# Two-layer decoder trunk: the last part of each feed-forward way down by eight products, chunk by chunk

## The chip, the cores and the metric

One core of one Trainium2 chip runs the whole program as a single launch. The metric is device microseconds of that core. The time before is the median of 3 runs; the profile is of one more execution.

## The reference, cut to what matters

The program computes two layers of a decoder trunk over 512 positions of width 1024, all in float32. Each layer adds to the residual x a mixer (layer 0: sliding-window and stick-breaking attention; layer 1: HGRN2, a gated linear recurrence), then a cross-attention to 256 memory rows, and then a feed-forward net. The change is in the last of these:

```python
def conv_ffn(h, w_up, conv_w, conv_b, w_down):
    S = h.shape[1]
    u = h @ w_up                                   # 1024 -> 2 * 2816
    shift = lambda t, n: jnp.pad(t, ((0, 0), (n, 0), (0, 0)))[:, :S]
    u = sum(conv_w[CONV_WIDTH - 1 - n] * shift(u, n) for n in range(CONV_WIDTH)) + conv_b
    gate, up = jnp.split(u, 2, axis=-1)
    return (jax.nn.silu(gate) * up) @ w_down       # 2816 -> 1024

for l in range(2):
    ...
    x = x + conv_ffn(rms_norm(x, norm_ffn[l]), ffn_w_up[l], ffn_conv_w[l], ffn_conv_b[l], ffn_w_down[l])
```

`h @ w_up` is the way up, `@ w_down` the way down. The inner width 2816 is 22 chunks of 128.

## The kernel before, in words

**Layout.** The residual lives transposed: `xT[c]` holds channels 128c to 128c+127 on the partitions and the 512 positions along the row (8 chunks; `xT2` joins two chunks in one tile). Every float32 operand of a product is split in two parts: `hi` (a cast to fp32r on ScalarE, `A.copy`) and `lo = x - hi` (on VectorE); see `split`. A product is then three matmuls: hi·hi, hi·lo and lo·hi (`mm3`, L183 to L185; in `seven_part` all three stand in L349).

**Weights.** `wload` loads a tile of 256 columns by DMA from SyncE's queue into `wraw` (two buffers), and splits it into `whi` and `wlo` (two buffers each) at L171 and L172. The buffers of one tile come free when the last matmul that reads them is done.

**Way up.** `ffn` walks over m = 0 to 10, two inner chunks at a time: `gate_half(m)` and `value_half(m)` each multiply the normed input with one weight tile (`proj_fm`: two outputs j = 0, 1 of 128x512 in the PSUM tile `ps_pj`, three buffers, 24 matmuls each, k in order). The evacuation of one output is `half`: times the row norm into `fu` (VectorE, L613), first tap and bias into `fa` (ScalarE, L615), two more taps (VectorE, L616 and L618); then the gate's Silu, or for the value the product with the gate (VectorE, L638).

**Way down.** The 22 inner chunks are cut into three parts, `parts = [(0, 8), (8, 16), (16, 22)]`, and after each part its share of the way down is added to the residual. It is done with seven block products in place of eight: the pair of chunks of one m and the two halves of 256 positions make a 2x2 block, `seven` builds the seven right operands of it (`s7h` and `s7l`, with sums in `s7t`; L318 to L321, and splits in L213 and L214), and `seven_part` builds the seven left operands from the weights (`wr`, `wraw`, sums in `wsum`, L353, splits L213 and L214), multiplies (L349: 128x128 by 128x256) into the PSUM tiles `ps_at`, `ps_ov` and `ps_pj`, and adds the results into `xT2` (`into`, L366). It does so in two units of four output chunks. For the last part (`fill` is false, since no gate half follows) the first unit takes another order of the seven products, with the last k held back.

**After the way down.** In layer 0 the next mixer follows. Its `norm` takes the chunks of xT one by one: scale and split into `xh` and `xl` (L235, L236, two instructions each, since this norm is folded), squares (ScalarE), their sum `nacc` (GpSimd, L246, the last one on VectorE); `Norm.finish` makes of the sum the factor of each position and spreads it by a matmul (L256, L266). The projections of the mixer read xh and xl chunk by chunk. At the same time GpSimd builds seven masks (L1075 to L1081). In layer 1 the way down is the end of the program: `store(sp, c)` transposes chunk c (TensorE, L436), copies it to `ot` (two buffers; ScalarE for even c, VectorE for odd, L441 and L439) and writes it out by DMA (L442).

**Order.** The framework orders each engine's instructions ahead of time with a planner of its own (`schedule_with_timeline_sim=True`): among the instructions that its reckoned times show as ready, it takes the earliest in the program. On the chip each engine then keeps that order.

`proj_resid`, which the attention's and the HGRN2's output projections use, is the plain way: for each of four weight tiles of 256 columns two outputs of 128x512, each the sum over all k, added to one chunk of xT (L297), and then, where given, a function `after(c)`.

Of the kernel before, what the change touches and what calls it, by code (L numbers as in the profile page):

```python
# [11 lines left out]
FP32R = mybir.dt.float32r  # L12
I32 = mybir.dt.int32
AF = mybir.ActivationFunctionType
ALU = mybir.AluOpType
# [3 lines left out]
P = 128  # L19
# [7 lines left out]
FC = DFF // P  # L27
# [6 lines left out]
def trunk(ctx, tc, x, mem, positions, norm_mix, norm_cross, norm_mem, norm_ffn,  # L34
# [13 lines left out]
    def tl(pool, shape, tag, bufs=1, dt=FP32):  # L48
        return pool.tile(shape, dt, name=tag, tag=tag, bufs=bufs)
# [22 lines left out]
    def f32(ap):  # L72
        return ap.bitcast(FP32)
# [138 lines left out]
    def split(src, hi, lo, eng=None):  # L212
        A.copy(out=hi, in_=src)  # L213
        V.tensor_tensor(out=lo, in0=src, in1=f32(hi), op=ALU.subtract)  # L214
# [109 lines left out]
        split(t, hi[:, 3:7], lo[:, 3:7])  # L324
        return hi, lo

    def seven_part(w, r0, xs, sp, sums, fill, after=None):


        n = len(xs)  # L330
        nk = 2 * n
        side = [None, 0]

        def weights(src):
            if side[1] == 0:
                side[0] = tl(wp, [P, KC, WCOL], "whi", 2, FP32R), tl(wp, [P, KC, WCOL], "wlo", 2, FP32R)
            h, lo = (t[:, side[1] * n:(side[1] + 1) * n] for t in side[0])
            side[1] = 1 - side[1]
            split(src, h, lo)
            return h, lo  # L340

        def product(o, wt, slot, first, ks=None):
            wh, wl = wt
            for k in range(n) if ks is None else ks:
                xh, xl = xs[k][0][:, slot], xs[k][1][:, slot]
                for j in range(2):
                    c = slice(j * P, (j + 1) * P)
                    for i, (p, q) in enumerate(((wh, xh), (wh, xl), (wl, xh))):
                        T.matmul(o[:, j], lhsT=p[:, k, c], rhs=q, start=first and k == 0 and j == 0 and i == 0,  # L349
                                 stop=k == n - 1 and j == 1 and i == 2, skip_group_check=True)  # L350

        def add(out, p, q):
            V.tensor_tensor(out=out, in0=p, in1=q, op=ALU.add)  # L353

        def unit(u, fill):
            raws = []
            for i in range(2):
                raw = tl(sp if i == 0 else wp, [P, KC, WCOL], "wr" if i == 0 else "wraw", 1 + i)
                SY.dma_start(out=raw[:, :nk], in_=wcols(w, r0, nk * P, (4 * u + 2 * i) * P))
                raws.append(raw)  # L360
            a11, a12 = (raws[0][:, i:nk:2] for i in range(2))
            a21, a22 = (raws[1][:, i:nk:2] for i in range(2))

            def into(i, th, o, op):
                x = xT2[2 * u + i][:, :, 256 * th:256 * th + 256]
                V.tensor_tensor(out=x, in0=x, in1=o, op=op)  # L366

            ws = tl(sp, [P, KC // 2, WCOL], "wsum", sums)[:, :n]
            al, be, de = ps("at", 2, WCOL), ps("ov", 2, WCOL), ps("pj", 2, WCOL)
            w11 = weights(a11)  # L370
            if not fill:
                w12 = weights(a12)
                product(al, w11, 0, True, range(n - 1))
                product(be, w12, 1, True, range(n - 1))
                product(al, w11, 0, True, range(n - 1, n))
                product(be, w12, 1, True, range(n - 1, n))
                add(ws, a21, a22)
                into(0, 0, al, ALU.add)
                into(0, 0, be, ALU.add)
                w1 = weights(ws)  # L380
                add(ws, ws, a11)
                w2 = weights(ws)
                product(al, w2, 4, False)
                product(de, w1, 3, True)
                add(ws, ws, a12)
                into(0, 1, al, ALU.add)
                into(1, 1, de, ALU.subtract)
                add(a21, a11, a21)
                w3 = weights(a21)
                w4 = weights(ws)  # L390
                product(al, w3, 5, False)
                product(de, w4, 2, False)
                w22 = weights(a22)
                into(1, 1, al, ALU.subtract)
                into(0, 1, de, ALU.add)
            else:
                add(ws, a21, a22)
                w1 = weights(ws)
                product(al, w11, 0, True)
                product(de, w1, 3, True)  # L400
                add(ws, ws, a11)
                w2 = weights(ws)
                into(0, 0, al, ALU.add)
                product(al, w2, 4, False)
                add(ws, ws, a12)
                w4 = weights(ws)
                into(1, 1, de, ALU.subtract)
                product(de, w4, 2, False)
                add(a21, a11, a21)
                w3 = weights(a21)  # L410
                into(0, 1, al, ALU.add)
                product(al, w3, 5, False)
                w12 = weights(a12)
                into(0, 1, de, ALU.add)
                product(be, w12, 1, True)
                w22 = weights(a22)
                into(1, 1, al, ALU.subtract)
                into(0, 0, be, ALU.add)
            product(al, w22, 6, False)
            if after is not None:  # L420
                for c in (4 * u, 4 * u + 1):
                    after(c)
            into(1, 0, al, ALU.subtract)
            if after is not None:
                for c in (4 * u + 2, 4 * u + 3):
                    after(c)

        unit(0, fill)
        unit(1, True)

    ov = out[0].rearrange("(t p) d -> p t d", p=P)

    def store(sp, c):
        pt = ps("at" if c % 2 else "tr", NT, P)
        for t in range(NT):
            T.transpose(out=pt[:, t], in_=xT[c][:, t * P:(t + 1) * P], identity=ident)  # L436
        ot = tl(sp, [P, NT, P], "ot", 2)
        if c % 2:
            V.tensor_copy(out=ot, in_=pt)  # L439
        else:  # L440
            A.copy(out=ot, in_=pt)  # L441
        SY.dma_start(out=ov[:, :, c * P:(c + 1) * P], in_=ot)  # L442
# [163 lines left out]
    def ffn(l, xp, sp):  # L606
        n = norm(gains("ffn", l), xtiles(xp))
        xh, xl, rb = n.xh, n.xl, n.rb
        parts = [(0, 8), (8, 16), (16, 22)]

        def half(o, ch):
            u = tl(sp, [P, S], "fu", 2)
            V.tensor_tensor(out=u, in0=o, in1=rb, op=ALU.mult)  # L613
            a = tl(sp, [P, S], "fa", 6)
            A.activation(out=a, in_=u, func=AF.Identity, scale=conv_col(l, 2, ch), bias=bias_col(l, ch))  # L615
            V.scalar_tensor_tensor(out=a[:, 1:], in0=u[:, :S - 1], scalar=conv_col(l, 1, ch), in1=a[:, 1:],  # L616
                                   op0=ALU.mult, op1=ALU.add)
            V.scalar_tensor_tensor(out=a[:, 2:], in0=u[:, :S - 2], scalar=conv_col(l, 0, ch), in1=a[:, 2:],  # L618
                                   op0=ALU.mult, op1=ALU.add)
            return a  # L620

        hs = {}

        def gate_half(m):
            gt = [None, None]

            def evg(j, o):
                a = half(o, 2 * m + j)
                A.activation(out=a, in_=a, func=AF.Silu)
                gt[j] = a  # L630
            wg = wload(wcols(ffn_w_up[l], 0, D, m * WCOL))
            proj_fm(wg, xh, xl, evg, n.finish if m == 0 else None, after_rows(n) if m == 0 else None)
            return gt

        def value_half(m, gt):
            def evu(j, o):
                a = half(o, FC + 2 * m + j)
                V.tensor_tensor(out=a, in0=gt[j], in1=a, op=ALU.mult)  # L638
                gt[j] = a
                if j:  # L640
                    hs[m] = seven(sp, sp, gt[0], gt[1], 4)
            wu = wload(wcols(ffn_w_up[l], 0, D, DFF + m * WCOL))
            proj_fm(wu, xh, xl, evu)


        gt = gate_half(0)
        for a, b in parts:
            for m in range(a // 2, b // 2):
                value_half(m, gt)
                gt = gate_half(m + 1) if 2 * m + 2 < FC else None  # L650
            seven_part(ffn_w_down[l], a * P, [hs[m] for m in range(a // 2, b // 2)], sp, 2 - l, gt is not None,
                       (lambda c: store(sp, c)) if l == 1 and b == FC else None)

    first_norm = []

# [601 lines left out]
    for l in range(2):  # L1257
# [3 lines left out]
        sp, sp_close = pool(f"xa{l}", "left")  # L1261
# [9 lines left out]
        sp, sp_close = pool(f"ffn{l}", "right")  # L1271
# [29 lines left out]
```

## Time and profile before

| what | value |
|---|---|
| runs | 1616.61, 1621.70, 1620.54 us; median 1620.54 |
| the profiled execution | 1618.11 us, its span 1616.3 us |
| TensorE clock granted, mean | 0.992 |
| TensorE (PE) busy | 1576.8 us, 98% |
| VectorE (DVE) busy | 1164.2 us, 72% |
| ScalarE (ACT) busy | 761.1 us, 47% |
| GpSimd (POOL) busy | 196.2 us, 12% |

All times inside the profile count from the start of the span. Busy TensorE time is the union of modelled matmul durations that overlap one another: matmuls start closer together than they last, so costs below are taken from the distance of their starts. "Granted clock" is the share of its full clock that TensorE was given in a stretch.

### The profile page before, as it was taken

How to read it: one execution, taken by the hardware profiler on the slowest of the kernel's cores; microseconds unless marked ns; L12 is line 12 of the kernel's file. 1: busy time of each engine (PE TensorE's matmuls, PEld its weight loads, DVE VectorE, ACT ScalarE, POOL GpSimd, SP SyncE). 2: the span in 40 equal slices, each digit the busy share in tenths (PEclk: the TensorE clock that was granted, in tenths of full speed). 3: DMA queues.
4: the chain of work that ended last, by engine and by line, in shares of the span. 5: the costliest groups of instructions: out<-in, count | busy, mean ns of one | idle time of the engine just before them, and what ended most of it. 6: DMA issues, size and time to landing. Idle time of an engine off the chain costs nothing.

```text
span 1616.3 us, 23124 instructions
## 1 busy us (share of the span) xinstructions
PE 1576.8 (98%) x9182; PEld 1363.9 (84%) x9182; DVE 1164.2 (72%) x1888; ACT 761.1 (47%) x1312; POOL 196.2 (12%) x307
## 2 busy tenths in 40 slices
PE   8999999999999999997999999999999999999997
PEld 7977898887888888987889888988888889889887
DVE  6766976566688779688776677645555988788786
ACT  6576874454443344344433344544543544444332
POOL 3302422002000000001322223101002000000000
PEclk9999999999999999998999999999999999999998
DMA  6211434213322421421322212342204322422312
GB/s 192 79 54 31 129 107 132 79 53 105 104 79 74 135 86 60 136 65 46 105 79 79 78 53 91 119 157 79 78 27 130 105 78 65 145 91 66 124 40 73
DMA packets 144489, 145.71 MB, mean 90 GB/s; under 512 B 2844, under 2 KB 143837, under 8 KB 144381
## 3 DMA queue, kind: packets, MB, share of 16 engines
q1 hardware_dynamic: 143882, 143.98, 27.9%
q8 instruction: 73, 1.20, 0.3%
q0 software_dynamic: 96, 0.07, 0.1%
q14 instruction: 35, 0.29, 0.1%
q10 hardware_dynamic: 403, 0.18, 0.0%
HBM read 142.12 MB, written 2.10 MB: 89 GB/s over the span
## 4 chain that ended last, share of the span: by engine, by line
PE 90%; DVE 4%; ACT 3%; DMA 1%; POOL 1%; issue 0%; SPq 0%; DVEq 0%; ACTq 0%
PE ps_pj L185 23%; PE ps_pj L184 23%; PE ps_pj L183 23%; PE ps_at L349 7%; PE ps_pj L349 3%; PE ps_ov L349 2%; PE ps_at L1123 1%; DVE wlo L214 1%; PE ps_ov L994 1%; ACT whi L213 1%; DVE xl L236 1%; DMA wraw<-in_ab_w_in_dram 1%; PE ps_tr L983 1%; PE ps_at L183 1%; PE ps_at L185 1%; DVE wlo L172 1%
## 5 line engine op out<-in xcount | busy, mean ns | idle before, releaser
L184 PE MATMUL ps_pj<-xl,whi 128*128 128x512 f32 x1088 | 430.5, 396 | 0.0
L185 PE MATMUL ps_pj<-xh,wlo 128*128 128x512 f32 x1024 | 408.5, 399 | 0.0
L183 PE MATMUL ps_pj<-xh,whi 128*128 128x512 f32 x1024 | 406.7, 398 | 0.0
L172 DVE TENSOR_TENSOR wlo<-wraw,whi 128x1024 fp32r<-128x1024 f32 (+1 forms) x228 | 264.2, 1191 | 45.8 <-ACT whi L171 45.2
L171 ACT CAST whi<-wraw 128x1024 fp32r<-128x1024 f32 (+1 forms) x228 | 219.5, 1012 | 161.1 <-PE ps_pj L184 107.9
L184 PEld LDWEIGHTS ps_pj<-xl,whi 128*128 128x128 f32 x1088 | 204.8, 188 | 49.6 <-issue 1.2
L183 PEld LDWEIGHTS ps_pj<-xh,whi 128*128 128x128 f32 x1024 | 192.7, 188 | 44.6 <-issue 1.2
L185 PEld LDWEIGHTS ps_pj<-xh,wlo 128*128 128x128 f32 x1024 | 192.6, 188 | 43.7
L615 ACT ACTIVATE fa<-fu,ccol 128x512 f32<-128x512 f32 x88 | 71.6, 814 | 100.7 <-DVE fu L613 100.5
L185 PE MATMUL ps_pj<-whi,xl 128*128 128x256 f32 x416 | 118.4, 287 | 0.1
L246 POOL TENSOR_TENSOR nacc<-nacc,nsq 128x512 f32<-128x512 f32 x36 | 50.6, 1406 | 540.9 <-ACT nsq L245 540.5
L349 PE MATMUL ps_at<-s7h,whi 128*128 128x256 f32 x352 | 102.7, 292 | 5.8 <-ACT s7h L213 3.4
L349 PE MATMUL ps_at<-s7l,whi 128*128 128x256 f32 x352 | 102.0, 290 | 1.5 <-DVE s7l L214 1.5
L349 PE MATMUL ps_at<-s7h,wlo 128*128 128x256 f32 x352 | 101.8, 290 | 1.3 <-DVE wlo L214 1.3
L184 PE MATMUL ps_pj<-ol,whi 128*128 128x512 f32 x256 | 101.7, 397 | 0.0
L183 PE MATMUL ps_pj<-oh,whi 128*128 128x512 f32 x256 | 99.9, 401 | 1.4 <-DVE xl L478 0.9
L185 PE MATMUL ps_pj<-oh,wlo 128*128 128x512 f32 x256 | 101.2, 397 | 0.0
L613 DVE TENSOR_TENSOR fu<-ps_pj,rb 128x512 f32<-128x512 f32 x88 | 60.7, 689 | 45.7 <-PE ps_pj L185 45.4
L183 PE MATMUL ps_pj<-whi,xh 128*128 128x256 f32 x288 | 82.8, 290 | 0.7 <-ACT xh L235 0.7
L184 PE MATMUL ps_pj<-wlo,xh 128*128 128x256 f32 x288 | 81.9, 286 | 0.0
L185 PEld LDWEIGHTS ps_pj<-whi,xl 128*128 128x128 f32 x416 | 78.5, 190 | 0.6 <-DVE xl L236 0.3
L349 PEld LDWEIGHTS ps_at<-s7h,whi 128*128 128x128 f32 x352 | 69.3, 197 | 7.8 <-ACT s7h L213 3.8
(382 smaller groups left out, 3279.8 us busy)
## 6 DMA issues: line engine op xcount, KB each, us to landing
wraw<-in_ffn_w_up_dram SPq DMA_DIRECT2D x44, 1024.0 KB, 5.1
wraw<-in_xa_w_kv_dram SPq DMA_DIRECT2D x16, 1024.0 KB, 6.0
wraw<-in_hgrn_w_in_dram SPq DMA_DIRECT2D x16, 1024.0 KB, 5.4
wraw<-in_ab_w_in_dram SPq DMA_DIRECT2D x8, 1024.0 KB, 5.4
wraw<-in_xa_w_q_dram SPq DMA_DIRECT2D x8, 1024.0 KB, 5.1
wraw<-in_xa_w_o_dram SPq DMA_DIRECT2D x8, 1024.0 KB, 5.0
wr<-in_ffn_w_down_dram SPq DMA_DIRECT2D x8, 1024.0 KB, 5.2
wraw<-in_ffn_w_down_dram SPq DMA_DIRECT2D x8, 1024.0 KB, 5.0
```

The lines of the kernel that those rows point to most:

```text
L171: A.copy(out=hi[:, k, c], in_=raw[:, k, c])
L172: V.tensor_tensor(out=lo[:, k, c], in0=raw[:, k, c], in1=f32(hi[:, k, c]), op=ALU.subtract)
L183: mm = T.matmul(o, lhsT=lh, rhs=rh, start=first, stop=False)
L184: T.matmul(o, lhsT=lh, rhs=rl, start=False, stop=False)
L185: T.matmul(o, lhsT=ll, rhs=rh, start=False, stop=last)
L213: A.copy(out=hi, in_=src)
L214: V.tensor_tensor(out=lo, in0=src, in1=f32(hi), op=ALU.subtract)
L236: self.last = V.scalar_tensor_tensor(out=b, in0=v, scalar=g, in1=f32(a), op0=ALU.mult, op1=ALU.subtract)
L246: (V if c == KC - 1 else G).tensor_tensor(out=self.acc, in0=self.acc, in1=sq, op=ALU.add)
L349: T.matmul(o[:, j], lhsT=p[:, k, c], rhs=q, start=first and k == 0 and j == 0 and i == 0, stop=k == n - 1 and j == 1 and i == 2, skip_grou ...
L613: V.tensor_tensor(out=u, in0=o, in1=rb, op=ALU.mult)
L615: A.activation(out=a, in_=u, func=AF.Identity, scale=conv_col(l, 2, ch), bias=bias_col(l, ch))
```

## The change

For the last part of each layer (inner chunks 16 to 21, m = 8, 9, 10) `value_half` no longer builds the seven operands; it splits each chunk as it comes into a tile of two chunks, and the way down of that part goes through `proj_resid` with those six chunks. In layer 1 `store` is called for each output chunk after its addition. Parts one and two keep the seven products, in the order that they had. The branch of `seven_part` for a last part, and its `after`, are gone.

```diff
-    def seven_part(w, r0, xs, sp, sums, fill, after=None):
+    def seven_part(w, r0, xs, sp, sums):
...
-            if not fill:
-                w12 = weights(a12)
-                product(al, w11, 0, True, range(n - 1))
-                product(be, w12, 1, True, range(n - 1))
-                product(al, w11, 0, True, range(n - 1, n))
-                product(be, w12, 1, True, range(n - 1, n))
...
-            else:
-                add(ws, a21, a22)
...
+            add(ws, a21, a22)
...
             product(al, w22, 6, False)
-            if after is not None:
-                for c in (4 * u, 4 * u + 1):
-                    after(c)
             into(1, 0, al, ALU.subtract)
-            if after is not None:
-                for c in (4 * u + 2, 4 * u + 3):
-                    after(c)
-
-        unit(0, fill)
-        unit(1, True)
+
+        unit(0)
+        unit(1)
...
                 a = half(o, FC + 2 * m + j)
                 V.tensor_tensor(out=a, in0=gt[j], in1=a, op=ALU.mult)
                 gt[j] = a
-                if j:
+                if m >= last:
+                    if j == 0:
+                        hs[m] = [tl(sp, [P, 7, 256], "s7" + c, 4, FP32R)[:, :4].rearrange("p (a b) c -> p a (b c)", a=2)
+                                 for c in "hl"]
+                    split(a, hs[m][0][:, j], hs[m][1][:, j])
+                elif j:
                     hs[m] = seven(sp, sp, gt[0], gt[1], 4)
...
+        last = parts[-1][0] // 2
         gt = gate_half(0)
         for a, b in parts:
             for m in range(a // 2, b // 2):
                 value_half(m, gt)
                 gt = gate_half(m + 1) if 2 * m + 2 < FC else None
-            seven_part(ffn_w_down[l], a * P, [hs[m] for m in range(a // 2, b // 2)], sp, 2 - l, gt is not None,
-                       (lambda c: store(sp, c)) if l == 1 and b == FC else None)
+            if b < FC:
+                seven_part(ffn_w_down[l], a * P, [hs[m] for m in range(a // 2, b // 2)], sp, 2 - l)
+            else:
+                hh, hl = ([hs[i // 2][q][:, i % 2] for i in range(a, b)] for q in range(2))
+                proj_resid(ffn_w_down[l], a * P, hh, hl, (lambda c: store(sp, c)) if l == 1 else None)
```

More of the change, by code (lines that the diff above doesn't have):

```diff
@@ L340, in weights, with product @@
             return h, lo
-        def product(o, wt, slot, first, ks=None):
+        def product(o, wt, slot, first):
             wh, wl = wt
-            for k in range(n) if ks is None else ks:
+            for k in range(n):
                 xh, xl = xs[k][0][:, slot], xs[k][1][:, slot]
@@ L353, in add, with unit @@
             V.tensor_tensor(out=out, in0=p, in1=q, op=ALU.add)
-        def unit(u, fill):
+        def unit(u):
             raws = []
@@ L370, in unit @@
             w11 = weights(a11)
-            if not fill:
-                w12 = weights(a12)
-                product(al, w11, 0, True, range(n - 1))
-                product(be, w12, 1, True, range(n - 1))
-                product(al, w11, 0, True, range(n - 1, n))
-                product(be, w12, 1, True, range(n - 1, n))
-                add(ws, a21, a22)
[L378 to L395, printed above, removed]
-            else:
[L397 to L418, printed above, removed]
@@ new lines, in unit @@
+            add(ws, a21, a22)
+            w1 = weights(ws)
+            product(al, w11, 0, True)
+            product(de, w1, 3, True)
+            add(ws, ws, a11)
+            w2 = weights(ws)
+            into(0, 0, al, ALU.add)
+            product(al, w2, 4, False)
+            add(ws, ws, a12)
+            w4 = weights(ws)
+            into(1, 1, de, ALU.subtract)
+            product(de, w4, 2, False)
+            add(a21, a11, a21)
+            w3 = weights(a21)
+            into(0, 1, al, ALU.add)
@@ L419, in unit @@
+            product(al, w3, 5, False)
+            w12 = weights(a12)
+            into(0, 1, de, ALU.add)
+            product(be, w12, 1, True)
+            w22 = weights(a22)
+            into(1, 1, al, ALU.subtract)
+            into(0, 0, be, ALU.add)
             product(al, w22, 6, False)
-            if after is not None:
-                for c in (4 * u, 4 * u + 1):
-                    after(c)
             into(1, 0, al, ALU.subtract)
-            if after is not None:
-                for c in (4 * u + 2, 4 * u + 3):
-                    after(c)
```

## The prediction

> **What bounds the kernel now.** I read the page first: the busy times (in the table above) and the chain that ended last.
>
> ```profile
> PE 90%; DVE 4%; ACT 3%; DMA 1%; POOL 1%; issue 0%; SPq 0%; DVEq 0%; ACTq 0%
> ```
>
> TensorE carries 90% of the chain, so a change pays by giving it less to do or fewer waits. Busy time can't say which, since matmuls overlap in it. So next the matmuls of L349 alone, over the two stretches in which the last part goes down (columns: stretch, length, PE busy and count, PEld, granted clock, DMA share, GB/s):
>
> ```profile
> 731.70:776.00 44.30, 36.02 (x252) 34.73 (x251) 0.85 0.21 66
> 1567.40:1607.60 40.20, 34.64 (x252) 32.97 (x251) 0.92 0.16 47
> ```
>
> Both hold the 252 matmuls of seven products (2 units x 7 x 3 pairs x 2 x 3), and neither had the full clock. What one costs when nothing waits is read from starts: in the timeline, the 97 starts of 128x512 matmuls from the first row below to the second; in the chain, a run of 18 of 128x256, then transposes and the end of the program.
>
> ```profile
> 1544.79 0.40 PE L185 MATMUL ps_pj<-xh,wlo 128*128 128x512 f32 x1
> ...
> 1567.19 0.40 PE L185 MATMUL ps_pj<-xh,wlo 128*128 128x512 f32 x1
> ```
>
> ```profile
> 1605.49 2.12 PE ps_at L349 x18
> 1607.61 0.44 PE ps_tr L436 x4
> ...
> 1609.24 2.72 DMA out_dram<-ot
> ...
> 1612.08 0.69 DVE ot L439
> ```
>
> A 512-wide matmul takes (1567.19 - 1544.79) / 96 = 0.2333 us, a 256-wide one 2.12 / 18 = 0.118, a transpose 0.11. The 252 should take 29.7 us. They take 44.3 in layer 0 and 40.2 in layer 1. The waits of TensorE (layer 0 with the start of the next mixer; layer 1; the start of an attention output projection) and the busy times by stage (PE, PEld, DVE, ACT, POOL, then the clock) show the rest:
>
> ```profile
> PE ps_pj L349 <- ACT whi L213: 4.3, 1, 4.3
> PE ps_at L349 <- ACT s7h L213: 2.5, 1, 2.5
> PE ps_tr L266 <- DVE nsq L263: 2.1, 1, 2.1
> ...
> PE ps_at L349 <- DVE wlo L214: 0.2, 1, 0.2
> ```
>
> ```profile
> PE ps_tr L436 <- DVE xT L366: 0.9, 1, 0.9
> ...
> PE ps_ov L349 <- ACT s7h L213: 0.5, 1, 0.5
> ```
>
> ```profile
> PE ps_pj L183 <- ACT oh L213: 0.2, 1, 0.2
> ```
>
> ```profile
> 415.00:427.00 12.00, 12.00 (x52) 9.33 (x51) 8.92 (x12) 7.77 (x9) 0.00 (x0) 1.00 0.19 60
> 676.00:731.70 55.70, 55.70 (x241) 44.79 (x239) 44.34 (x62) 23.16 (x31) 0.00 (x0) 1.00 0.24 80
> 743.00:757.00 14.00, 13.32 (x91) 13.17 (x91) 10.35 (x15) 6.56 (x11) 1.32 (x1) 0.77 0.30 98
> 757.00:770.00 13.00, 8.52 (x53) 8.11 (x52) 11.01 (x15) 5.17 (x10) 2.81 (x3) 0.74 0.06 13
> 792.00:804.00 12.00, 10.32 (x36) 7.60 (x37) 9.21 (x20) 5.13 (x9) 2.24 (x6) 0.86 0.02 5
> 1567.40:1579.50 12.10, 8.97 (x67) 8.03 (x65) 11.87 (x18) 5.61 (x7) 0.00 (x0) 0.98 0.20 65
> 1579.50:1590.40 10.90, 10.85 (x66) 10.60 (x67) 7.63 (x10) 2.40 (x3) 0.00 (x0) 0.71 0.01 2
> 1607.60:1616.30 8.70, 1.89 (x17) 1.50 (x14) 2.07 (x3) 1.17 (x2) 0.00 (x0) 0.82 0.44 121
> ```
>
> The first fence has six rows with 10.4 us, of which 8.3 lie in the way down (2.1 is the next norm's); the second five rows with 4.0. After each series of waits the clock falls: 0.77 of 14 us and 0.74 of 13 us lose 3.2 + 3.4 us, 0.86 of 12 us loses 1.7, 0.71 of 10.9 us loses 3.2. Layer 0 adds up: 29.7 + 8.3 + 6.6 = 44.6. Layer 1: 29.7 + 16 transposes 1.8 + 4.0 + 3.2 = 38.7 of 40.2; 1.5 are in gaps too short to be listed. While TensorE waits, DVE is full: 11.87 of 12.1 us.
>
> **Why it waits there.** Rows of VectorE and ScalarE around the last value chunk:
>
> ```profile
> 1562.03 0.69 DVE L613 TENSOR_TENSOR fu<-ps_pj,rb 128x512 f32<-128x512 f32 x1 [0.88 <-PE ps_pj L185]
> ...
> 1565.17 0.69 DVE L638 TENSOR_TENSOR fa<-fa 128x512 f32<-128x512 f32 x1
> ...
> 1572.60 0.95 DVE L214 TENSOR_TENSOR wlo<-wsum,whi 128x768 fp32r<-128x768 f32 x1
> ...
> 1578.28 1.22 DVE L214 TENSOR_TENSOR s7l<-s7t,s7h 128x1024 fp32r<-128x1024 f32 x1
> ```
>
> ```profile
> 1570.86 0.83 ACT L213 CAST whi<-wsum 128x768 fp32r<-128x768 f32 x1 [1.69 <-DVE wsum L353]
> 1572.72 0.62 ACT L213 CAST s7h<-fa 128x512 fp32r<-128x512 f32 x1 [1.03 <-DVE fa L638]
> ```
>
> An undisturbed evacuation takes 3.8 us from fu to the end of the product with the gate. The last chunk's starts at 1567.6, but its last operand is done at 1579.5: sums and weight splits of 0.95 us stand between. That is what the products wait for.
>
> **The change part by part.**
>
> *Matmuls, both layers.* Out: 252 of 256 wide. In: 8 outputs x 6 k x 3 = 144 of 512 wide, 144 x 0.2333 = 33.6 us. Against 29.7 that is 3.9 us more work in each layer. It stands only against the 44.3 and 40.2 that the seven products really take.
>
> *Vector work, both layers.* Out: 8 sums and 14 splits of weights at 0.95 and 14 additions at 0.69, 30.6 us of DVE, and the operands of three m; in: 8 splits at 0.95 and 8 additions at 0.69, 13.1 us. It costs nothing as long as it lies beside matmuls. Each weight tile feeds 36 matmuls, 8.4 us, in which the next one's two splits (1.9 us DVE, 1.7 ACT) and two additions (1.4) fit. If that cover went, one tile would cost TensorE up to 3.6 us. In the way up before it, TensorE is full (55.70 of 55.70), so fewer operands to build there bring nothing.
>
> *Start of the way down, the term without a row.* The sum over k ends with the last chunk, and that comes 3.8 + 0.2 for the semaphores + 0.62 = 4.6 us after the last value matmul, 5.3 with its lo. Cover: 15 matmuls of the first output (k = 0 to 4) are 3.5 us, 15 of the second 3.5 more, 7.0 in all, and a third PSUM buffer holds the next tile's. The nearest row is the attention output projection, which also waits for its last k: 0.2 us. Bounds: 0, and 4.6 - 3.5 = 1.1 with a slow clock behind (up to 3.2), 4.3. I take 0.4 a layer, nearest to that row. Below nothing is excluded: this wait can't be less than none.
>
> *Layer 0, the next norm.* Chunks 0 to 6 are now finished 4.2 us apart, not four at a time, so their scaling, squares and sums on GpSimd lie beside matmuls. The wait of 2.1 us and the slow clock behind it, 1.7, should go. GpSimd still builds masks there, which can delay the row factors. The nearest row is the feed-forward norm behind an output projection in eight products: 415 to 427 is full at clock 1.00 (that norm isn't folded: half as many scalings). Bounds: gain 3.8, gain 0. I take 3.4, near that row.
>
> *Layer 1, the stores.* Seven chunks' transposes are in the stream: 7 x 0.44 = 3.1 us (four before). Each needs its addition first; the row of before shows one such wait of 0.9. Bounds 0 to 7 x 0.9 = 6.3; I take 0.15 each, 1.0, since DVE is now idle half of the time and matmuls of the next chunk can go ahead. The tail: now 8.7 us, because four chunks' copies queue for two `ot` buffers, and the last copy waits for a DMA of 2.72. Then, chunk 6 is stored 4.2 us ahead, and after the last matmul come: addition 0.1 + 0.69, transposes 0.6, copy 0.69, DMA 2.7, and 0.8 from there to the end of the span (1616.3 - 1612.77 - 2.7), 5.6.
>
> *Queues.* SyncE issues four 768 KB loads as before, now all into `wraw`. The third tile's can go once the first has been split, 8.4 us and more before its use, against this landing time:
>
> ```profile
> wraw<-in_ffn_w_down_dram SPq DMA_DIRECT2D x4, 768.0 KB, 4.4
> ```
>
> So they are hidden; a load queued behind a store of `ot` could be late by that store's wait, but the last load is due before the first store. GpSimd gets the same sums, earlier. `ps_at`, which the stores use, is no longer shared with products.
>
> *The sum.* Layer 0: -44.3 + 33.6 + 0.4 = -10.3, norm -3.4. Layer 1: -40.2 + 33.6 + 3.1 + 0.4 + 1.0 = -2.1, tail 5.6 - 8.7 = -3.1. In all -18.9. From the profiled execution's 1618.1 us that is 1599.2; it was 2.4 below the median of 1620.5, and from there it is 1601.6. I take 1600.
>
> **The rivals.**
>
> *A, the sum above.* 1600, with its own range of 1595 to 1605.
>
> *B, the last chunk's wait stays.* If TensorE's order keeps output after output, each layer waits 1.1 us and pays the slow clock, 4.3 in place of 0.4: +7.8, 1608. For it: the clock fell to 0.71 in layer 1 behind waits of at most 0.9. Against: the row of 0.2 in the same situation. The Trainium skill ("TensorE: Matmul & The Clock Gate", the table of what matters for kernels) says that only idle gaps over about 3 us bring the half clock back; by that rule B would cost 0.7 a layer more than A, 1601, inside A's range. This trace disagrees: 0.71 stands behind waits of 0.9 us, and the measurement decides.
>
> *C, the ends gain nothing.* The norm still waits (+3.4), and each store's transposes wait 0.9 (+5.3): 1609. For it: masks on GpSimd, the row of 0.9. Against: DVE is no longer full.
>
> *D, slower: the weights become the bound.* Each of the 8 weight tiles must be split within 8.4 us behind norm and store work on ScalarE and VectorE. If the planner puts the splits last, a tile is late by its two splits, 3.6 us, and its matmuls run at 0.74 clock behind (8.4 / 0.74 - 8.4 = 3.0): 8 x 6.6 = 53 us, 1652. It decides at 18.9 / 8 = 2.4 us per tile. Against: splits and additions are 3.3 us of 8.4 on VectorE, before two chunks' norm or stores; and 415 to 427, which ends an output projection of the same shape with larger tiles and runs into the next weights, is full.
>
> *E, no change.* The stalls come back in the order of the next mixer, whose instructions are all planned anew: all of 18.9 would have to return. Nothing in the rows speaks for it.
>
> **How the numbers follow.** A 0.74, B 0.10, C 0.08, D 0.04, E 0.04. The runs shown spread over 0.3% (1616.6 to 1621.7), about what can be told from no change; faster by more means under 1615.7. A, B and C are faster: 0.92; E 0.04; D 0.04. The range reaches from A's low end, less 2 us for waits that I don't list, to C: 1593 to 1609, which leaves out D, E and the tails.
>
> **What would show it.** In the changed profile: 288 matmuls of 512 in place of 504 of 256; the last part of layer 0 takes about 34 us at clock 1.00, with a first wait of under 1 us; no wait of L266 for nsq; TensorE's last matmul to the end of the span 5.6 us. I am wrong if TensorE waits several us for the last chunk or for `wlo`, if a slow clock shows in these stretches, or if the mixer of layer 1 takes longer than now.

## The result, and the profile after

| | before | after |
|---|---|---|
| median | 1620.39 us (4 runs, 1616.61 to 1621.70) | 1600.52 us (4 runs, 1599.90 to 1604.62) |
| ratio | | 0.9887, 95% interval 0.9863 to 0.9910 |
| profiled execution, span | 1618.11, 1616.3 us | 1600.87, 1599.2 us |
| mean granted clock | 0.992 | 0.998 |

The change makes the kernel 20 us faster. First the page of the changed kernel, TensorE's busy time and the chain that ended last:

```profile
PE 1575.4 (99%) x8966; PEld 1352.3 (85%) x8966; DVE 1121.5 (70%) x1818; ACT 745.1 (47%) x1294; POOL 199.3 (12%) x307
...
PE 94%; ACT 2%; DVE 1%; DMA 1%; issue 0%; POOL 0%; SPq 0%
```

TensorE's busy time is almost the same (1576.8 before); what went are 4 points of the chain's share on VectorE and ScalarE, and the slow clock of these stages. The stages (length, busy time of PE, PEld, DVE, ACT, POOL, then clock, DMA share and GB/s): way down of layer 0, the start of the next norm, on to the first score matmul, way down of layer 1, tail.

```profile
733.10:767.00 33.90, 33.90 (x146) 27.06 (x146) 25.53 (x35) 17.40 (x31) 7.71 (x5) 1.00 0.35 108
767.00:776.00 9.00, 9.00 (x40) 7.26 (x39) 6.17 (x12) 4.76 (x7) 7.57 (x16) 1.00 0.47 150
776.00:791.40 15.40, 15.40 (x71) 12.22 (x70) 9.25 (x18) 4.89 (x9) 4.47 (x17) 1.00 0.05 9
1556.60:1593.50 36.90, 36.90 (x172) 29.79 (x171) 15.44 (x23) 7.61 (x11) 0.00 (x0) 1.00 0.22 64
1593.50:1599.20 5.70, 1.05 (x8) 0.57 (x6) 1.38 (x2) 0.59 (x1) 0.00 (x0) 0.83 0.32 92
```

TensorE is full in the first four and has its full clock. Where the last part's 0.85 and 0.92 stood there is 1.00. The chain shows how the last chunk's lateness was covered; three first terms of a product in a row, in layer 0 and in layer 1:

```profile
744.09 0.70 PE ps_pj L183 x3
...
1567.58 0.70 PE ps_pj L183 x3
```

These are the sixth k of three outputs at once. They stand 10.7 us after the first matmul of the way down (733.38 and 1556.87), and 45 matmuls of 0.2333 us are 10.5: TensorE had done five of six k for three outputs, one for each PSUM buffer. That is the order that the planner chose, and more cover than was needed: in layer 1 the last chunk's split ends at 1563.09, 6.2 us after the first matmul of the way down and 4 us before its turn (the same 6.2 in layer 0), so two outputs, 7.0 us, would have done. On VectorE this last split begins 5.3 us after the chunk's fu, though two weight splits (1557.71) still stand between:

```profile
1557.07 0.69 DVE L581 TENSOR_TENSOR fu<-ps_pj,rb 128x512 f32<-128x512 f32 x1 [0.38 <-PE ps_pj L185]
1557.71 1.83 DVE L172 TENSOR_TENSOR wlo<-wraw,whi 128x768 fp32r<-128x768 f32 x2
...
1562.40 0.69 DVE L214 TENSOR_TENSOR s7l<-fa,s7h 128x512 fp32r<-128x512 f32 x1 [0.69 <-ACT s7h L213]
```

Stage by stage, from the starts of matmuls in the traces (us):

| stage | before | after | change |
|---|---|---|---|
| start of the program to the way down of the last part, layer 0 | 731.7 | 733.4 | +1.7 |
| that way down, to the first projection of the next mixer | 44.25 | 33.84 | -10.4 |
| on to the first score matmul | 28.02 | 24.17 | -3.85 |
| on to the way down of the last part, layer 1 | 763.5 | 765.5 | +2.0 |
| that way down with its stores, first to last matmul | 39.9 | 36.2 | -3.7 |
| tail to the end of the span | 9.0 | 6.1 | -2.9 |
| span | 1616.3 | 1599.2 | -17.1 |

The +1.7 lies ahead of the change and isn't its doing: the same stretch took 733.6 in a kernel whose layer 0 is unchanged (layer 1 alone, below). The +2.0 is in the mixer of layer 1. TensorE's waits around 990 us there:

```profile
PE ps_tr L1116 <- POOL hK L1106: 1.7, 1, 1.7
PE ps_at L1101 <- ACT KM L1098: 1.0, 1, 1.0
```

Before, the like place had 1.8 us of waits, of which 0.6 were for hK, and the full clock. Behind these waits the clock is at half for 3.4 us (columns as above):

```profile
980.00:989.70 9.70, 7.71 (x46) 6.30 (x44) 6.65 (x12) 4.82 (x11) 4.59 (x6) 1.00 0.12 42
989.70:993.10 3.40, 2.74 (x13) 2.74 (x14) 3.26 (x10) 1.91 (x5) 1.02 (x2) 0.50 0.81 247
```

The 0.9 us of further waits and half of the 2.74 us, 1.4, come to about the 2 us. With layer 0 alone changed (below) the same place has 3.1 us of waits and no slow clock.

### The profile page after: what moved, and what is told of

Read it like the earlier page. It is cut to its first block, busy times and chain, and to the rows that moved or that the text cites. A ratio compares the mean times of both kernels' runs of the same rounds, so it can differ in the third digit from the quotient of the medians.

```text
span 1599.2 us, 22607 instructions
## 1 busy us (share of the span) xinstructions
PE 1575.4 (99%) x8966; PEld 1352.3 (85%) x8966; DVE 1121.5 (70%) x1818; ACT 745.1 (47%) x1294; POOL 199.3 (12%) x307
## 4 chain that ended last, share of the span: by engine, by line
PE 94%; ACT 2%; DVE 1%; DMA 1%; issue 0%; POOL 0%; SPq 0%
PE ps_pj L185 25%; PE ps_pj L184 25%; PE ps_pj L183 25%; PE ps_at L349 6%; PE ps_pj L349 3%; PE ps_at L1101 2%; PE ps_ov L349 1%; PE ps_ov L972 1%; DMA sbqk<-in_x_dram 1%; PE ps_tr L961 1%; PE ps_at L183 1%; PE ps_at L185 1%; PE ps_at L184 1%; ACT whi L213 1%; PE ps_ov L1133 0%; PE ps_at L1081 0%
## 5 line engine op out<-in xcount | busy, mean ns | idle before, releaser
L172 DVE TENSOR_TENSOR wlo<-wraw,whi 128x1024 fp32r<-128x1024 f32 (+2 forms) x244 | 281.0, 1185 | 44.9 <-ACT whi L171 44.2
L171 ACT CAST whi<-wraw 128x1024 fp32r<-128x1024 f32 (+2 forms) x244 | 232.1, 1001 | 165.2 <-PE ps_pj L184 114.1
L584 DVE SCALAR_TENSOR_TENSOR fa<-fu,ccol,fa 128x511 f32<-128x511 f32 x88 | 65.5, 747 | 14.9 <-ACT fa L583 14.9
L349 PE MATMUL ps_at<-s7h,whi 128*128 128x256 f32 x256 | 72.5, 283 | 1.6 <-ACT whi L213 0.9
L349 PE MATMUL ps_at<-s7h,wlo 128*128 128x256 f32 x256 | 71.9, 282 | 1.1 <-DVE wlo L214 1.1
L349 PE MATMUL ps_at<-s7l,whi 128*128 128x256 f32 x256 | 72.0, 281 | 0.0
```

The costliest lines, as they stand in the source:

```text
L171: A.copy(out=hi[:, k, c], in_=raw[:, k, c])
L172: V.tensor_tensor(out=lo[:, k, c], in0=raw[:, k, c], in1=f32(hi[:, k, c]), op=ALU.subtract)
```

## The experiments

Theory: the gain is made in each layer's last part and at its end, because a sum over k that ends with the late chunk lets TensorE run ahead, while seven products wait for operands that a full VectorE makes. Rivals: most of it is the stores, or the lighter VectorE as such. Every ratio below is against the kernel before, run beside that experiment; where there is one run only, the stages of its trace are compared.

**Layer 0 alone**

```diff
-                if j:
+                if l == 0 and m >= 8:
+                    ...   # split(a, hs[m][0][:, j], hs[m][1][:, j])
+                elif j:
...
+            if l == 0 and b == FC:
+                proj_resid(ffn_w_down[l], a * P, hh, hl, ...)
+            else:
+                seven_part(..., gt is not None, ...)   # as before
```

> The kernel before with the change in layer 0 alone. My theory, that each layer's gain is made in its own last part and at its end: layer 0 gains 14.2 us (way down 44.3 to 33.8, next norm 28.0 to 24.2), layer 1 keeps its 48.9 us from the first product of the last part to the end; the time is 14 us below the kernel before, 12 if the mixer of layer 1 again takes 2 us longer. Rival, that the gain is mostly at the end of the program (stores chunk by chunk): under 7 us.

1608.37 us against 1620.38, ratio 0.9924 (0.9908 to 0.9940): 12.0 us. Way down 33.84, on to the score matmul 24.17, as in the changed kernel; the next stretch 765.1, so the 2 us of the mixer come with layer 0's change; layer 1 takes 40.8 + 9.0 (39.9 + 9.0 before).

**Layer 1 alone**

The same edit with `l == 1`.

> The kernel before with the change in layer 1 alone. My theory: 6.6 us below the kernel before (way down with stores 40.0 to 36.4, tail 8.9 to 5.9), and the mixer of layer 1 as before, since nothing ahead of it changes. Rival, that the stores are most of the whole gain: over 12 us.

1612.77 us, ratio 0.9954 (0.9937 to 0.9970): 7.6 us. Way down 36.2, tail 6.1, the mixer 763.3 as before. The two add up to 19.6 of the 20 us: little is left for any other place, and the stores aren't most of it.

**Output after output**

```diff
+        def place(mm):                       # first matmul of each k
+            seen.append(mm)
+            if len(seen) > nk and len(seen) % nk == 1:
+                behind(mm, seen[-2])         # after the start of the last k of the output before
...
-            proj_fm(wt, xh, xl, lambda j, o: evac(2 * mm + j, o))
+            proj_fm(wt, xh, xl, lambda j, o: evac(2 * mm + j, o), place=place if in_order else None)
```

> The changed kernel, but in the last part TensorE must finish an output before it starts the next. My theory, that the last chunk's lateness is covered only because TensorE runs ahead into the next outputs: a wait of 1 to 2 us after 15 matmuls in each layer, with up to 3.2 us of slow clock behind: 2 to 10 us above the changed kernel. Rival, that fewer vector instructions alone bring the last chunk in time: no wait, no difference.

1606.90 us, ratio 0.9916 (0.9900 to 0.9932), and a span of 1603.8 against 1599.2. TensorE's wait, the same row in both layers, and the stage around it in layer 0:

```profile
PE ps_pj L183 <- ACT s7h L213: 1.9, 1, 1.9
```

```profile
733.00:745.00 12.00, 10.13 (x44) 7.87 (x43) 6.08 (x9) 3.07 (x5) 0.00 (x0) 1.00 0.21 67
745.00:768.00 23.00, 23.00 (x100) 18.50 (x99) 18.34 (x27) 14.36 (x27) 6.94 (x5) 1.00 0.39 120
```

So the wait is real and TensorE's running ahead is what covers it: ways down 35.85 and 38.25, 2.0 and 2.1 longer. No slow clock followed. The kernel stays 13.5 us below the one before, so running ahead is the smaller part of the gain, about 2 us a layer in the trace (6.4 in all by the medians).

**All three parts by eight**

```diff
-                if m >= last:
+                if True:
...
-            if b < FC:
+            if False:
...
```

> All three parts by eight products. My theory, that seven products pay wherever TensorE is kept fed: parts one and two take 192 x 0.2333 = 44.8 us each in place of 41.6 on the mean, four times, so 12.6 us above the changed kernel and 5 below the kernel before. Rival, that the vector work of seven products is what costs everywhere: not above the changed kernel.

1614.42 us, ratio 0.9963 (0.9948 to 0.9978); span 14.2 above the changed kernel. Each of parts one and two took 44.75 us from first to last matmul, against 41.25 to 41.8 with seven, though VectorE had little left to do (columns as above):

```profile
505.00:550.00 45.00, 45.00 (x194) 36.19 (x193) 16.39 (x18) 9.36 (x11) 0.00 (x0) 1.00 0.29 94
```

A lighter VectorE is worth nothing where TensorE is fed; there seven products stay cheaper.

**Seven products without the weight sums** (one run)

```diff
+        last = n == 3                        # pairs of chunks: three in the last part alone
...
-            ws = tl(sp, [P, KC // 2, WCOL], "wsum", sums)[:, :n]
+            ws = tl(sp, [P, KC // 2, WCOL], "wsum", sums)[:, :n] if not last else a21
...
         def add(out, p, q):
+            if last:
+                return
```

> The kernel before with the sums of weight blocks left out in the last parts (raw blocks are split in their place; the results of those parts are therefore other numbers): 8 instructions of 0.95 us less on VectorE in each layer, and no chain through them. My theory, that the last chunk's operands come late because VectorE is full of weight work: the lost time (44.3 and 39.9 against 29.7 and 31.5 without waits) shrinks by at least a third, and the last s7l comes 2 us or more earlier after the last value matmul than the 12 us of before. Rival, that the operands' own chain is what takes so long: the waits for s7h and s7l stay as they are.

1608.61 us; ways down 34.3 in layer 0 (44.3) and 35.5 in layer 1 (39.9). The last operand, which began 10.9 us after the last value matmul before (1567.4 to 1578.28), begins 7.6 us after it here (1562.4):

```profile
1563.23 1.83 DVE L214 TENSOR_TENSOR wlo<-wraw,whi 128x768 fp32r<-128x768 f32 x2
...
1569.96 1.23 DVE L214 TENSOR_TENSOR s7l<-s7t,s7h 128x1024 fp32r<-128x1024 f32 x1 [0.51 <-ACT s7h L213]
```

The theory's expectation holds: eight sums of 0.95 us on VectorE, 7.6 us in each layer, and the chain through them cost TensorE 9.9 us in layer 0 and 4.4 in layer 1.

**Seven products that don't wait for the last chunk** (one run)

```diff
-            seven_part(ffn_w_down[l], a * P, [hs[m] for m in range(a // 2, b // 2)], ...)
+            seven_part(ffn_w_down[l], a * P, [hs[min(m, 9)] for m in range(a // 2, b // 2)], ...)
```

> The kernel before, but in the last parts the products read the operands of m = 9 in place of m = 10 (so m = 10 adds nothing of its own; its operands are still built): no product waits for the last chunk. If the last chunk's operands are the cause: the waits for s7h and s7l vanish and with them the slow clock, way down under 36 us in layer 0 and under 35 in layer 1. If the weight splits behind a full VectorE are the cause: the waits for whi and wlo stay (4.3 us the longest in layer 0) and the way down stays over 39 in layer 0.

1612.29 us; ways down 39.9 and 36.8. The waits for s7h and s7l are gone; in layer 0 this stays, with a clock of 0.87 behind it:

```profile
PE ps_pj L349 <- ACT whi L213: 6.3, 2, 3.9
```

```profile
757.00:770.00 13.00, 9.13 (x60) 8.59 (x59) 10.17 (x14) 4.37 (x8) 3.00 (x2) 0.87 0.19 61
```

By the bounds set ahead the last chunk alone is not the cause: layer 0 stays over 39 us with its wait for whi, layer 1 over 35, and the slow clock does not go. Both causes are there. Not waiting for the last chunk is worth 4.3 and 3.1 us, leaving the sums out 9.9 and 4.4; the two overlap, since the sums also delay that chunk.

**Stores after the whole way down** (one run)

```diff
-                proj_resid(ffn_w_down[l], a * P, hh, hl, (lambda c: store(sp, c)) if l == 1 else None)
+                proj_resid(ffn_w_down[l], a * P, hh, hl)
+                for c in range(KC if l == 1 else 0):
+                    store(sp, c)
```

> The changed kernel, with the eight stores behind the whole way down of layer 1 in the program. My theory, that the tail is set by two output buffers and the stores left over: 3.0 us of transposes leave the way down (36.2 to 33.4), and the tail grows from 6.1 to about 17 (four rounds of copy and DMA, some 3.5 us each, and the end): 8 us above the changed kernel. Rival, that stores overlap among themselves: within 3 us of it.

1607.56 us: way down 34.3, tail 14.8, together 6.8 us above the changed kernel (8 expected). The end of the chain is a queue for two `ot` buffers, 3.2 us a round:

```profile
1595.25 0.70 DVE ot L407
1595.95 0.02 issue
1595.96 2.35 DMA out_dram<-ot
...
1598.44 0.70 DVE ot L407
```

**Norm of four chunks held until the last** (one run)

```diff
+            V.scalar_tensor_tensor(out=n.late[:, :8], in0=xT[7][:, :8], scalar=0.0, in1=gcols, op0=ALU.mult, op1=ALU.add)
+            ...                                  # and eight ones, the same way
-            g = self.g[:, c:c + 1]
+            g = (self.late if self.late is not None and c >= 4 else self.g)[:, c:c + 1]
...
+                    A.activation(out=sq, in_=xT[c], func=AF.Square, scale=self.late[:, 8:9])
```

> The changed kernel, but in the norm at the start of the mixer of layer 1 the scaling and squares of chunks 4 to 7 wait for the last chunk's addition (their factors are read from a tile that is made from it), as they came in the kernel before. My theory, that 3.8 us of layer 0's gain are the norm chunk by chunk: from the end of the way down to the first score matmul 24.2 becomes about 28, with a wait for the row factors. Rival, that the masks on GpSimd set that time: 24.2 stays.

1605.95 us; from the way down to the first score matmul 30.1 in place of 24.2. That is 2 us more than the 28.0 of the kernel before too, so this holds the chunks back harder than that kernel did. The wait of before is back, longer, and the slow clock with it:

```profile
PE ps_tr L270 <- DVE nsq L267: 3.5, 1, 3.5
```

```profile
780.00:793.00 13.00, 9.46 (x35) 6.99 (x34) 6.14 (x14) 3.37 (x5) 3.70 (x14) 0.74 0.00 0
```

The masks run on GpSimd here as there, so they alone don't set the 24.2; when the chunks come does.

**Weight sums on GpSimd, two kernels**

```diff
         def add(out, p, q):
-            V.tensor_tensor(out=out, in0=p, in1=q, op=ALU.add)
+            (G if n == 3 else V).tensor_tensor(out=out, in0=p, in1=q, op=ALU.add)   # in the kernel before
+            G.tensor_tensor(out=out, in0=p, in1=q, op=ALU.add)                      # in the changed kernel
```

> The kernel before with the weight sums of the last parts on GpSimd, which does nothing there. If VectorE full of sums is the cause of the lost time, most of what leaving the sums out brought comes back with the true result: way down 36 to 40 us in layer 0 (34.3 without sums, 44.3 before) and 36 to 38 in layer 1 (35.5 and 39.9), 1606 to 1614 in all; still above the changed kernel, since the ends stay as before (tail 9.0). If GpSimd's sums, at 1.5 times the 1.4 us of its 512-wide ones some 2.1 us each, come too late in their chain: no gain over the kernel before.

> The changed kernel with the weight sums of parts one and two on GpSimd. Those parts take 41.3 to 41.8 us against 39.6 without waits; if VectorE's load is what they lose, up to 1.5 us each, four times, 6 us below the changed kernel. If a chain of three sums at some 2.8 us (1024 wide) is what the products then wait for: 0 to 10 us above it.

The first: 1621.74 us, ratio 1.0021 (1.0008 to 1.0033), ways down 43.35 and 40.2: no gain. The second: 1624.33 us, ratio 1.0036 (1.0024 to 1.0047), that is 24 us above the changed kernel, its parent, where 10 at most were expected; the parts take 46.7 to 48.3 in place of 41.25 to 41.8. Both could have beaten their parents; neither did. GpSimd's rows and VectorE's in the first, side by side:

```profile
733.97 2.30 POOL L353 TENSOR_TENSOR wsum<-wsum,wr 128x768 f32<-128x768 f32 x1 [12.37 <-DVE wlo L214]
```

```profile
734.61 2.21 DVE L618 SCALAR_TENSOR_TENSOR fa<-fu,ccol,fa 128x510 f32<-128x510 f32 x1
736.74 0.68 DVE L366 TENSOR_TENSOR xT<-xT,ps_at 128x512 f32<-128x512 f32 x1
```

The tap takes 2.21 us where it took 0.75, and ends 0.55 us after the sum (736.27 and 736.82). So the sum leaves VectorE's list and is paid there all the same, and it takes 2.3 us here, 2.0 in the median, in place of 0.95. Which of the two costs more was not separated.

## Why the prediction was right, step by step

- *Start of the way down.* Forecast 0.4 a layer; measured 0. The nearest row, 0.2, was the right neighbour. The last chunk's hi came 5.5 us after the last value matmul, not 4.6, because two weight splits stood between; the two outputs that I counted on, 7.0 us, would still have covered it, and TensorE ran ahead by three.
- *Matmuls.* Forecast 33.6; layer 0 took 33.84. That eight products cost more work and less time stands.
- *Next norm.* Forecast -3.4, measured -3.85: the wait of 2.1 and the slow clock's 1.7 both went, as the forecast's upper bound had it.
- *Stores.* Forecast 1.0 of waits; measured one of 0.3, after the last matmul. Six chunks' transposes stand in the way down, not the seven of the forecast: those of chunk 6 come at 1593.29, behind the last matmul, so it is not stored 4.2 us ahead. With that and the start at 0, layer 1's way down fell by 3.7, where 2.1 was forecast. The tail: -2.9 for a forecast of -3.1.
- *What I left out.* +2.0 in the mixer of layer 1. A longer mixer was among the signs of being wrong that the prediction named, and it came; the sum had no term for it. From the first score matmul to the first of layer 1's three ways down it is 534.3 us before, in layer 1 alone, and where only the operands that are read differ; in every kernel here whose layer 0 has other instructions in its last part it is 535.9 to 538.0, seven products with sums on GpSimd among them (536.6). That points to the planner's order of the mixer, which is made anew, but is not shown; what in the order causes it was not tried. My terms came to -18.9; with what was really saved, -20.9, the +2.0 and the +1.7 of the program's start give the span's -17.1. The fit of 1600 is therefore in part luck of opposite signs, each within 2 us.
- *Rival B* would have been 2.0 a layer, not 3.9: its wait was 1.9, not 1.1, and the slow clock that I added did not come. It did come behind waits of 2.0 and 2.1 us in other kernels here (last section), so why it stayed away is open. *C* failed on both ends. *D* never began: VectorE is busy for 15.4 of 36.9 us in layer 1's way down.
- *Cause of the old stall.* I put it down to the last chunk's operands, late because sums and splits on VectorE stand between its steps. That is the smaller part: the products that don't wait for that chunk at all gain 4.3 and 3.1 us. The larger part goes with the sums, which the weight operands wait for too (the waits for whi stay in that kernel): without sums, seven products took 34.3 us in layer 0, about what eight take. The forecast didn't hang on it, since it took the 44.3 and 40.2 as measured and both parts go with the change. My 6.6 us of slow clock in layer 0 are about 1 us too many, since they count time in which TensorE waited: it is busy for 4.72 of the 6.80 us from 763.20 on.

## What to carry to other kernels

A scheme with fewer multiplications pays only where the engine that prepares its operands has time; price it by what its stage takes in the trace, not by its matmuls alone, and decide part by part (here seven for parts one and two, eight for the last). Where the last operand comes late, a plain sum that ends with it lets TensorE run ahead by as many outputs as there are PSUM buffers: count that cover in us against the lateness (here worth 2 us a layer). Work that can follow each output, such as a norm or a store, then lies beside matmuls: that saved 3.85 us after layer 0 and 2.9 at the end, not more than the 3.9 us a layer that the further matmuls cost. The rest of the gain is time that the stages themselves lost before.

## What the runs showed of the hardware

*Sums on GpSimd stop VectorE.* An instruction with two inputs in SBUF that comes up while GpSimd's sum runs waits for it; one that takes an input from PSUM doesn't. From the changed kernel with all sums on GpSimd, GpSimd first:

```profile
509.11 2.84 POOL L353 TENSOR_TENSOR wsum<-wsum,wr 128x1024 f32<-128x1024 f32 x1 [7.92 <-DVE wlo L214]
```

```profile
509.61 0.68 DVE L366 TENSOR_TENSOR xT<-xT,ps_at 128x512 f32<-128x512 f32 x1
510.21 2.28 DVE L586 SCALAR_TENSOR_TENSOR fa<-fu,ccol,fa 128x510 f32<-128x510 f32 x1
```

Within the 2.84 us the addition from PSUM takes its usual 0.68; the tap after it, with both inputs in SBUF, needs 2.28 and ends 0.54 after the sum. The Trainium skill ("SBUF — State Buffer", Terms) says that VectorE and GpSimd arbitrate for a shared port pair, held for a whole instruction, and that the loser "fully blocks"; this trace agrees.

*When the clock falls.* The 0.71 to 0.87 of the tables above are means: in the traces the slow clock is 0.50, over stretches of some 3.4 or 6.8 us inside the program. How long the wait ahead of it was doesn't settle whether it comes. Single waits of 1.9 us (output after output, twice) left the clock at 1.00, and so did one of 2.5 us (layer 0, without the last chunk). But 2.1 us of waiting for nsq in the kernel before and 2.0 us in layer 1 without the last chunk were each followed by 3.4 us at half clock, 3.5 us (norm held) by 6.9 us. The one of 2.0 us, as its row of waits and the stretches before and at the slow clock (columns as above):

```profile
PE ps_pj L349 <- ACT whi L213: 2.0, 1, 2.0
```

```profile
1567.00:1576.90 9.90, 7.89 (x67) 7.65 (x66) 9.90 (x17) 4.83 (x6) 0.00 (x0) 1.00 0.05 11
1576.90:1580.30 3.40, 3.40 (x19) 3.40 (x18) 2.94 (x4) 0.71 (x2) 0.00 (x0) 0.50 0.61 200
```

The Trainium skill ("TensorE: Matmul & The Clock Gate", the table of what matters for kernels) asks for "No PE-idle gaps >~3µs between matmul bursts". The waits of 3.5 us and more agree with it; those of 2.0 and 2.1 us show that staying below it isn't enough here. And in the kernel before, layer 1, waits of at most 0.9 us, 3.1 us of idle time in 12.1, were followed by 0.71: several short waits can do what one long one does. How close they must lie was not tried.
